# Odd attention: low keys padded with zero rows to 128, and the key latent's projection moved ahead of the compression MLP

## The chip, the cores and the metric

The kernel runs on one core of one Trainium2 chip. Its time is the device time of one execution in microseconds (us). Five engines work side by side, each through its own list of instructions in order: TensorE (PE) multiplies matrices into PSUM banks, with a second stream (PEld) that loads its weights; VectorE (DVE) and ScalarE (ACT) do the elementwise work; GpSimd (POOL) helps; SyncE (SP) issues the DMAs.

## What is computed

The program is two blocks on 256 tokens of width 1024 in fp32. Only one part of the second block is touched, the odd layer's mixer. Cut to what matters:

```python
def odd_mixer(x, w_in, w_out, cmp_pe, cmp_w1, cmp_w2, q_norm_g, kv_norm_g, w_uq, w_uk, w_uv, bias_table):
    q_c, kv_c, gate_c, cq, ckv, k_rope = split_cols(x @ w_in, ODD_SPLITS)
    q = q_c.reshape(B, S, G, Hg, C_DIM)              # G = 2 groups of Hg = 4 heads of 64
    kv = kv_c.reshape(B, S, 3, 2, G, C_DIM)
    o_cmp, slc_score = nsa_compressed(q, kv[:, :, 0, 0], kv[:, :, 0, 1], cmp_pe, cmp_w1, cmp_w2, tbl_c)
    o_slc = nsa_selected(q, kv[:, :, 1, 0], kv[:, :, 1, 1], slc_score, tbl_c)
    o_win, _ = banded_attention(q, kv[:, :, 2, 0], kv[:, :, 2, 1], WIN_SIZE - 1, tbl_c, 1)
    o_c = gates[:, :, 0] * o_cmp + gates[:, :, 1] * o_slc + gates[:, :, 2] * o_win
    qd = (rms_norm(cq, q_norm_g) @ w_uq).reshape(B, S, D_HEADS, D_NOPE + D_ROPE)
    c = rms_norm(ckv, kv_norm_g)
    k_nope, v = (c @ w_uk), (c @ w_uv)
    o_d = mla_attention(qd[..., :D_NOPE], rope(qd[..., D_NOPE:], pos), k_nope, rope(k_rope, pos), v)
    return jnp.concatenate([o_c, o_d], axis=-1) @ w_out
```

`nsa_compressed` runs a small MLP (gelu) over blocks of 32 keys, and one over blocks of 32 values, ahead of its attention.

## The kernel before

Activations lie with features on the partitions and tokens along the row. Every fp32 value that TensorE multiplies is split into a high part (rounded to the fast type) and a low part (the rest), and a product is three matmuls: high by high, low by high, high by low (L328 to L330, in `fm_mm`; L337 to L339 for the token-major form). A weight comes by DMA into a ring of raw tiles; ACT casts its high part (L320) and DVE subtracts for the low part (L321).

A scheduler places each instruction on its engine's list: of those that it reckons ready it takes the one of highest priority, and priority falls in the order in which the code makes them. The steps of the odd mixer are functions in a table, called in the order of the string `ORDER`: kv0, ks and q project keys, values and queries; c0 and c1 are the compression MLP for keys and values (`cmp_mlp`, passes L1387, its fold L1393, the last product of c0 L1408 and of c1 L1416); tm is the token-major projection of values and gates (`tmproj`); ckv projects the key latent and prepares its norm (`ckvproj`: copy L1509, then `rms_defer`, which scales on ACT, L568, squares on ACT, L491, sums the squares on PE, L454, takes the mean on ACT, L503, the power of -1/2 on POOL, L505, and spreads the result over the partitions by PE, L498); kr and cq do the same for the rotary key and the query latent (`cqproj`: copies L1522). CS0 to CS3 are the scores and softmax of pair i of heads (`c_scores`), CO0 to CO3 their outputs (`c_out`, transposes L947, products L1136 and L1138, the first of them preceded by `compressed`); uk, uv, uq are the up-projections from the latents; DS and DO the latent attention.

A score in `c_scores` is two matmuls per group g of heads and half t of the tokens. The tiles `QS[g]` hold the high part of the queries in one half of the partitions and the low part in the other; `KH[g]` holds the high keys twice, in both halves. L1468 multiplies them over 128 rows. L1469 adds high queries by low keys: the low keys KL of both groups lie in one tile, group g in its own 64 partitions, so this matmul runs over 64 rows. The columns are the keys of two branches (selected and window), 2 x 128 of them for the first half of the tokens and 2 x 256 for the second. So each pair of heads has eight matmuls, four of 256 and four of 512 columns. DVE adds the bias and takes the extreme (L1128, called from `biased`), ACT takes the exponential (L1475), DVE scales (L1484).

Tiles of the same tag share memory. The softmax of the second half (t = 1) writes tiles tagged csb1, and so do the first two weight tiles of c0 and c1: who comes later waits. The tile `te` of the query norm has the tag oks, that of KL. The query latent's tile `cq` has the tag ocq alone. PSUM has eight banks: three for projections (tag g), four for scores and transposes (tag a), one for all else (tag m).

Of the kernel before, what the change touches and what calls it, by code (L numbers as in the profile page):

```python
# [13 lines left out]
F32R = mybir.dt.float32r  # L14
# [6 lines left out]
P = 128  # L21
# [10 lines left out]
WPRI = 300  # L32
NRAW = 7
NRMS = 12
ORDER = ("kv0 ks q c0 tm ckv c1 CS0 CS1 CO0 CS2 CO1 CS3 CO2 kr CO3 cq uk uv uq DS0 DS1 DO0 DS2 DO1 DS3 "
         "DO2 DO3").split()
EORDER = ("aq av keep AS0 AS1 AO0 AO1 bq0 bq1 bq2 BS0 bv1 BS1 an bv0 bv2 BO0 BO1").split()
RA = 4
# [220 lines left out]
def _program(ctx, tc, nc, a, offs, dump):  # L259
# [17 lines left out]
    def T(pl, shape, tag, dt=F32, **k):  # L277
        cnt[0] += 1
        return pl.tile(list(shape), dt, tag=tag, name="%s_%d" % (tag, cnt[0]), **k)
# [11 lines left out]
    ident = C["ident"]  # L291
    ones = T(cp, [P, P], "ones")
    G.memset(ones, 1.0)
    mhalf = T(cp, [P, 8], "mhalf")
    G.memset(mhalf, -0.5)
    ebase = T(cp, [P, 16], "ebase")
# [2 lines left out]
    def bc(ap, shape):  # L299
        return ap.to_broadcast(list(shape))  # L300
# [1005 lines left out]
    def odd(ap_, xh, xl, W, KO, raw):  # L1306
# [1 line left out]
        X2 = T(ap_, [P, 2, 2, S], "s4")  # L1308
        X = [X2[:, j] for j in range(2)]
        KH = [T(ap_, [P, 2, S], "okh%d" % g, F32R) for g in range(2)]  # L1310
        KL = T(ap_, [P, 2, S], "oks", F32R)
        grp = (slice(0, 64), slice(64, 128))

        def evc(j, ps):
            if j == 1:
                for g in range(2):
                    for r in range(2):
                        ACT.copy(KH[g][grp[r]], ps[grp[g]])
                    tt(KL[grp[g]], ps[grp[g]], KH[g][grp[g]], op=sub)
                return  # L1320
            for u in range(2):
                V.tensor_copy(X[u][0:64, 0, :], ps[0:64, u, :])
                ACT.copy(X[u][64:128, 0, 0:S - 1], ps[0:64, u, 1:S])
                V.tensor_copy(X[u][0:64, 1, :], ps[64:128, u, :])
                ACT.copy(X[u][64:128, 1, 0:S - 1], ps[64:128, u, 1:S])
# [132 lines left out]
        def c_scores(i):  # L1458
# [4 lines left out]
            for t in range(2):  # L1463
                n = P * (t + 1)
                sps = [T(pa, [P, 2, S], "a") for g in range(2)]
                for g in range(2):
                    qt = QS[g][:, i, t * P:(t + 1) * P]
                    mm(sps[g][:, :, :n], qt, KH[g][:, :, 0:n], start=True, stop=False)  # L1468
                    mm(sps[g][:, :, :n], qt[grp[g]], KL[grp[g], :, 0:n], start=False, stop=True)  # L1469
                sb = T(ap_, [P, 2, 2, n], "csb%d" % t, bufs=2)  # L1470
                for g in range(2):
                    for b in range(2):
# [29 lines left out]
                             pT[g]) for g in range(2)], False, b == 1)  # L1502
            split(back(o), halves(yh[:, i, :]), halves(yl[:, i, :]))

        cq = T(ap_, [P, 3, S], "ocq")
        kr = T(ap_, [P, S], "okr")

        def evk(j, ps):
# [6 lines left out]
            late["k"] = rms_defer(ckv, 2, C["kv_norm"], 1e-5, ckx[:, 0], ckx[:, 1], (pg,))  # L1515

        def cqproj():
            late["cqx"] = cqx = [T(ap_, [P, 3, S], "ocx", F32R, bufs=2) for _ in range(2)]
            for n in range(3):
                ps = T(pg, [P, S], "g")  # L1520
# [279 lines left out]
```

## Time and profile before

| | us |
|---|---|
| median of 3 runs (lowest to highest) | 1218.49 (1217.42 to 1223.27) |
| the profiled execution | 1222.49 |
| its span | 1220.7 |
| PE busy in it | 1175.4 (96%) |
| DVE, ACT, POOL busy | 905.4, 681.7, 94.5 |
| the odd mixer, from the first matmul of kv0 to the final projection's last stretch | 888.28 to 999.94 |

The profile is of one execution. The span is what the profiler saw; the execution's own time has some 2 us around it. Each row of a timeline starts with its start in us from the span's begin and its length in us. A matmul's length includes the way through the array, so two matmuls that follow each other overlap: the price of one is the distance from its start to the next start. In a window's row, PEclk is the share of the full TensorE clock that was granted.

### The profile page before, as it was taken

How to read it: one execution, taken by the hardware profiler on the slowest of the kernel's cores; microseconds unless marked ns; L12 is line 12 of the kernel's file. 1: busy time of each engine (PE TensorE's matmuls, PEld its weight loads, DVE VectorE, ACT ScalarE, POOL GpSimd, SP SyncE). 2: the span in 40 equal slices, each digit the busy share in tenths (PEclk: the TensorE clock that was granted, in tenths of full speed). 3: DMA queues.
4: the chain of work that ended last, by engine and by line, in shares of the span. 5: the costliest groups of instructions: out<-in, count | busy, mean ns of one | idle time of the engine just before them, and what ended most of it. 6: DMA issues, size and time to landing. Idle time of an engine off the chain costs nothing.

```text
span 1220.7 us, 23603 instructions
## 1 busy us (share of the span) xinstructions
PE 1175.4 (96%) x9370; PEld 1111.6 (91%) x9370; DVE 905.4 (74%) x1744; ACT 681.7 (56%) x1205; POOL 94.5 (8%) x94
## 2 busy tenths in 40 slices
PE   7779999999999999999999899999999999999997
PEld 7769989999999999899998899998977789999986
DVE  8998957866689886667564886666687758976654
ACT  5345564755566765446355675554675566755541
POOL 4830000100000000000001000001000001000010
PEclk9979999999999999999999899999998999999998
DMA  7423445664356556656423556566754215666561
GB/s 262 139 87 114 147 137 179 205 202 157 100 177 196 183 177 181 196 175 215 163 79 106 170 173 187 176 181 190 261 182 139 70 54 193 208 188 188 160 201 36
DMA packets 61276, 199.41 MB, mean 163 GB/s; under 512 B 8502, under 2 KB 12398, under 8 KB 60910
## 3 DMA queue, kind: packets, MB, share of 16 engines
q1 hardware_dynamic: 54864, 191.60, 49.5%
q10 hardware_dynamic: 6302, 6.32, 1.6%
q8 instruction: 73, 1.20, 0.4%
q14 instruction: 37, 0.30, 0.1%
HBM read 196.28 MB, written 1.60 MB: 162 GB/s over the span
## 4 chain that ended last, share of the span: by engine, by line
PE 82%; DVE 11%; ACT 2%; DMA 2%; issue 2%; SPq 0%; DVEq 0%; ACTq 0%
PE g L329 10%; PE g L328 10%; PE g L330 10%; PE a L328 7%; PE a L329 7%; PE a L330 7%; PE a L393 5%; PE g L393 4%; DVE lo L321 3%; PE a L395 3%; PE g L337 2%; PE g L339 2%; PE g L338 2%; PE g L395 2%; PE a L947 1%
## 5 line engine op out<-in xcount | busy, mean ns | idle before, releaser
L321 DVE TENSOR_TENSOR lo<-raw,hi 128x1024 fp32r<-128x1024 f32 (+3 forms) x359 | 431.2, 1206 | 180.7 <-ACT hi L320 178.0
L320 ACT CAST hi<-raw 128x1024 fp32r<-128x1024 f32 (+3 forms) x359 | 363.7, 1020 | 355.4 <-PE g L329 138.8
L328 PE MATMUL g<-xh,hi 128*128 128x256 f32 (+1 forms) x616 | 176.2, 287 | 7.9 <-ACT xh L568 7.6
L329 PE MATMUL g<-xl,hi 128*128 128x256 f32 (+1 forms) x624 | 178.9, 287 | 0.3 <-DVE xl L569 0.3
L330 PE MATMUL g<-xh,lo 128*128 128x256 f32 (+1 forms) x616 | 176.3, 287 | 2.7 <-DVE lo L321 2.7
L328 PE MATMUL a<-nh,hi 128*128 128x256 f32 x560 | 159.9, 286 | 4.6 <-ACT sqa L1061 2.7
L329 PE MATMUL a<-nl,hi 128*128 128x256 f32 x560 | 159.5, 285 | 0.9 <-DVE nl L516 0.9
L330 PE MATMUL a<-nh,lo 128*128 128x256 f32 x560 | 159.3, 285 | 0.0
L328 PEld LDWEIGHTS g<-xh,hi 128*128 128x128 f32 x616 | 117.7, 191 | 9.9 <-ACT xh L568 7.9
L330 PEld LDWEIGHTS g<-xh,lo 128*128 128x128 f32 x616 | 117.4, 191 | 4.4 <-DVE lo L321 3.4
L329 PEld LDWEIGHTS g<-xl,hi 128*128 128x128 f32 x624 | 119.0, 191 | 1.4 <-DVE xl L569 0.9
L328 PEld LDWEIGHTS a<-nh,hi 128*128 128x128 f32 x560 | 108.6, 194 | 5.7 <-ACT sqa L1061 2.9
L329 PEld LDWEIGHTS a<-nl,hi 128*128 128x128 f32 x560 | 108.7, 194 | 1.1 <-DVE nl L516 1.1
L330 PEld LDWEIGHTS a<-nh,lo 128*128 128x128 f32 x560 | 108.7, 194 | 0.0
L393 PE MATMUL a<-mx,hi 128*128 128x512 f32 x264 | 91.9, 394 | 0.0
L328 PE MATMUL g<-nh,hi 128*128 128x256 f32 x288 | 81.5, 283 | 0.0
L329 PE MATMUL g<-nl,hi 128*128 128x256 f32 x288 | 81.5, 283 | 0.0
L330 PE MATMUL g<-nh,lo 128*128 128x256 f32 x288 | 81.5, 283 | 0.0
L395 PE MATMUL a<-mx,lo 128*128 128x256 f32 x264 | 73.1, 277 | 0.0
L393 PE MATMUL g<-mx,hi 128*128 128x512 f32 x198 | 69.0, 395 | 0.0
L393 PEld LDWEIGHTS a<-mx,hi 128*128 128x128 f32 x264 | 49.4, 188 | 11.5
L328 PEld LDWEIGHTS g<-nh,hi 128*128 128x128 f32 x288 | 55.3, 192 | 0.0
(619 smaller groups left out, 2905.2 us busy)
## 6 DMA issues: line engine op xcount, KB each, us to landing
raw<-g_up SPq DMA_DIRECT2D x88, 512.0 KB, 3.6
raw<-f_up SPq DMA_DIRECT2D x44, 512.0 KB, 3.5
raw<-g_dn SPq DMA_DIRECT2D x32, 512.0 KB, 3.6
raw<-w_fm SPq DMA_DIRECT2D x27, 512.0 KB, 4.1
raw<-ev_fm SPq DMA_DIRECT2D x20, 512.0 KB, 3.7
raw<-f_dn SPq DMA_DIRECT2D x16, 512.0 KB, 3.6
raw<-od_fm SPq DMA_DIRECT2D x14, 512.0 KB, 4.2
raw<-g_dn SPq DMA_DIRECT2D x16, 384.0 KB, 3.4
```

The lines of the kernel that those rows point to most:

```text
L320: ACT.copy(hi, raw)
L321: tt(lo, raw, hi, op=sub)
L328: mm(ps, hi[:, o:o + P], xh[:, k, :], start=start and k == 0, stop=False, skip_group_check=skip)
L329: mm(ps, hi[:, o:o + P], xl[:, k, :], start=False, stop=False, skip_group_check=skip)
L330: mm(ps, lo[:, o:o + P], xh[:, k, :], start=False, stop=stop and k == kt - 1, skip_group_check=skip)
L337: mm(ps, xh[:, k, t], hi[:, wsl], start=start and j == 0, stop=False, skip_group_check=skip)
L338: mm(ps, xh[:, k, t], lo[:, wsl], start=False, stop=False, skip_group_check=skip)
L339: mm(ps, xl[:, k, t], hi[:, wsl], start=False, stop=stop and j == len(ks) - 1, skip_group_check=skip)
L393: mm(f2, hi[:, o], X[:, k].rearrange("p a s -> p (a s)"), start=first and j == 0, stop=False, skip_group_check=True)
L395: mm(ps[:, 0, :], lo[:, o], X[:, k, 0, :], start=False, stop=last and j == len(ks) - 1, skip_group_check=True)
L947: PE.transpose(tr[:, k, :], b, ident)
```

## The change

Two things are changed, both in the odd mixer. First, the low keys get one tile per group (tags oks and ocq) of 128 rows, the other 64 of which ACT fills once with zeros, and L1469 multiplies the whole query tile by them, as L1468 does. Since the second of these tiles has the tag ocq, `cq` shares its memory with it, and is therefore made inside `cqproj`. Second, ckv stands ahead of c0 in `ORDER`. All lines from there on shift by two to four (L1468 is L1472 after, L498 is L500).

```diff
@@ -32,7 +32,7 @@
 WPRI = 300
 NRAW = 7
 NRMS = 12
-ORDER = ("kv0 ks q c0 tm ckv c1 CS0 CS1 CO0 CS2 CO1 CS3 CO2 kr CO3 cq uk uv uq DS0 DS1 DO0 DS2 DO1 DS3 "
+ORDER = ("kv0 ks q ckv c0 tm c1 CS0 CS1 CO0 CS2 CO1 CS3 CO2 kr CO3 cq uk uv uq DS0 DS1 DO0 DS2 DO1 DS3 "
          "DO2 DO3").split()
 EORDER = ("aq av keep AS0 AS1 AO0 AO1 bq0 bq1 bq2 BS0 bv1 BS1 an bv0 bv2 BO0 BO1").split()
 RA = 4
@@ -291,6 +291,8 @@
     ident = C["ident"]
     ones = T(cp, [P, P], "ones")
     G.memset(ones, 1.0)
+    zero = T(cp, [P, 1], "zero")
+    G.memset(zero, 0.0)
     mhalf = T(cp, [P, 8], "mhalf")
     G.memset(mhalf, -0.5)
     ebase = T(cp, [P, 16], "ebase")
@@ -1308,15 +1310,17 @@
         X2 = T(ap_, [P, 2, 2, S], "s4")
         X = [X2[:, j] for j in range(2)]
         KH = [T(ap_, [P, 2, S], "okh%d" % g, F32R) for g in range(2)]
-        KL = T(ap_, [P, 2, S], "oks", F32R)
+        KL = [T(ap_, [P, 2, S], tag, F32R) for tag in ("oks", "ocq")]
         grp = (slice(0, 64), slice(64, 128))
+        for g in range(2):
+            ACT.copy(KL[g][grp[1 - g]], bc(zero[grp[1 - g], None, :], [64, 2, S]))
 
         def evc(j, ps):
             if j == 1:
                 for g in range(2):
                     for r in range(2):
                         ACT.copy(KH[g][grp[r]], ps[grp[g]])
-                    tt(KL[grp[g]], ps[grp[g]], KH[g][grp[g]], op=sub)
+                    tt(KL[g][grp[g]], ps[grp[g]], KH[g][grp[g]], op=sub)
                 return
             for u in range(2):
                 V.tensor_copy(X[u][0:64, 0, :], ps[0:64, u, :])
@@ -1466,7 +1470,7 @@
                 for g in range(2):
                     qt = QS[g][:, i, t * P:(t + 1) * P]
                     mm(sps[g][:, :, :n], qt, KH[g][:, :, 0:n], start=True, stop=False)
-                    mm(sps[g][:, :, :n], qt[grp[g]], KL[grp[g], :, 0:n], start=False, stop=True)
+                    mm(sps[g][:, :, :n], qt, KL[g][:, :, 0:n], start=False, stop=True)
                 sb = T(ap_, [P, 2, 2, n], "csb%d" % t, bufs=2)
                 for g in range(2):
                     for b in range(2):
@@ -1502,7 +1506,6 @@
                              pT[g]) for g in range(2)], False, b == 1)
             split(back(o), halves(yh[:, i, :]), halves(yl[:, i, :]))
 
-        cq = T(ap_, [P, 3, S], "ocq")
         kr = T(ap_, [P, S], "okr")
 
         def evk(j, ps):
@@ -1515,6 +1518,7 @@
             late["k"] = rms_defer(ckv, 2, C["kv_norm"], 1e-5, ckx[:, 0], ckx[:, 1], (pg,))
 
         def cqproj():
+            cq = T(ap_, [P, 3, S], "ocq")
             late["cqx"] = cqx = [T(ap_, [P, 3, S], "ocx", F32R, bufs=2) for _ in range(2)]
             for n in range(3):
                 ps = T(pg, [P, S], "g")
```

Three places of the order of instructions. Names carry numbers that the program gives its tiles; a is a bank for scores, g one for projections, m the last one, csb softmax or MLP weights, ow the MLP's input.

TensorE, from head pair 1's last scores. Before:

```order
L1468 MATMUL a_11096<-okh_1628_10437,xh_10619 128x512
L1469 MATMUL a_11096<-oks_10438,xh_10619 128x512
L1387 MATMUL m_10988<-csb_1731_10989,ow_1650_10533 32x256 x4
L1387 MATMUL m_10988<-csb_1732_10995,ow_1650_10533 32x256 x4
L1387 MATMUL m_10988<-raw_11001,ow_1650_10533 32x256 x4
L1387 MATMUL m_10988<-raw_11007,ow_1650_10533 32x256 x3
L498 MATMUL g_10983<-consts_91,rmsr_10981 128x128 x2
L1387 MATMUL m_10988<-raw_11007,ow_1650_10533 32x256
```

After:

```order
L456 MATMUL g_10848<-ones_92,sq_1701_10849 128x1 x2
L456 MATMUL g_10848<-ones_92,sq_1702_10851 128x1 x2
L1472 MATMUL a_11099<-okh_1628_10438,xh_10623 128x512
L1473 MATMUL a_11099<-oks_10440,xh_10623 128x512
L1472 MATMUL a_11100<-okh_1629_10439,xh_10623 128x512
L1473 MATMUL a_11100<-ocq_10441,xh_10623 128x512
L500 MATMUL g_10861<-consts_91,rmsr_10859 128x128 x2
L339 MATMUL g_10914<-hi_10918,oh_10323 128x280
L340 MATMUL g_10914<-lo_10919,oh_10323 128x280
L341 MATMUL g_10914<-hi_10918,ol_10324 128x280
```

Before, c1's passes follow the scores, and the spread of the latent's rstd (L498) stands near their end; after, it follows the scores at once (L500), and the token-major projection (L339 to L341) follows it.

TensorE, around c1's last product (L1416 before, L1420 after). Before:

```order
L329 MATMUL g_11485<-ol_10322,hi_11488 128x256
L330 MATMUL g_11485<-oh_10321,lo_11489 128x256
L454 MATMUL g_11523<-ones_92,sq_1837_11524 128x1 x2
L454 MATMUL g_11523<-ones_92,sq_1838_11526 128x1 x2
L1416 MATMUL m_11031<-cod_10317,okr_11029 128x64 x2
L1453 MATMUL a_11146<-consts_91,ow_1758_11121 128x128 x2
L947 MATMUL a_11153<-consts_91,csb_1746_11043 128x128
L947 MATMUL a_11153<-consts_91,csb_1749_11058 128x128 x2
```

After:

```order
L330 MATMUL g_11458<-oh_10323,hi_11461 128x256
L331 MATMUL g_11458<-ol_10324,hi_11461 128x256
L332 MATMUL g_11458<-oh_10323,lo_11462 128x256
L1438 MATMUL a_11129<-okc_10446,s_1665_10622 128x32 x8
L1397 MATMUL m_11019<-cod_10319,okr_11017 128x32 x2
L1420 MATMUL m_11035<-cod_10319,okr_11033 128x64 x2
L1457 MATMUL a_11150<-consts_91,ow_1759_11125 128x128 x2
L949 MATMUL a_11157<-consts_91,csb_1747_11047 128x128
```

Before, 96 projection matmuls of the rotary key and query latent stand between c1's passes and this place; after, 57 of them stand ahead of c1's passes, 15 between these and this place, and 24 behind it.

ScalarE, from the latent's squares to its mean. Before (L491 squares, L503 mean):

```order
L491 ACTIVATE sq_1724_10971<-ockv_10903 128x256
L491 ACTIVATE sq_1725_10973<-ockv_10903 128x256
L1475 ACTIVATE csb_1746_11043,cden_11036<-csb_1746_11043,cnm_11035 128x128 x2
L320 CAST hi_11456<-raw_11454 128x1024
L1475 ACTIVATE csb_1746_11043,cden_11036<-csb_1746_11043,cnm_11035 128x128 x2
L1475 ACTIVATE csb_1754_11086,cden_11079<-csb_1754_11086,cnm_11078 128x128
L503 ACTIVATE rmsms_10979<-g_10970 128x2
```

After (L493 squares, L505 mean):

```order
L493 ACTIVATE sq_1702_10851<-ockv_10781 128x256
L322 CAST hi_11352<-raw_11350 128x1024
L1479 ACT_TABLE_LOAD
L1479 ACTIVATE csb_1747_11047,cden_11040<-csb_1747_11047,cnm_11039 128x128 x4
L1367 CAST xh_10623<-s_1665_10622 64x512 x2
L322 CAST hi_11429<-raw_11427 128x1024
L1479 ACTIVATE csb_1755_11090,cden_11083<-csb_1755_11090,cnm_11082 128x128
L505 ACTIVATE rmsms_10857<-g_10848 128x2
```

A cast of a weight, the load of the exponential's table, the casts of the last queries (L1367) and a second weight cast have come between the squares and the mean. Further on, the three copies of the query latent stand behind the last scores of head pair 3 on PE, because of the shared tag.

## Rows read from the trace of the kernel before

**Rows 1.** The page: the chain of work that ended last, by engine.

```profile
PE 82%; DVE 11%; ACT 2%; DMA 2%; issue 2%; SPq 0%; DVEq 0%; ACTq 0%
```

**Rows 2.** Windows: length, busy us of PE, PEld, DVE, ACT, POOL; PEclk; DMA.

```profile
888.28:905.97 17.69, 17.38 (x158) 16.13 (x157) 15.62 (x35) 12.92 (x24) 2.60 (x3) 1.00 0.67 236
909.70:923.40 13.70, 12.31 (x60) 7.24 (x60) 10.53 (x43) 9.94 (x34) 0.71 (x1) 0.50 0.57 163
938.34:962.06 23.72, 23.72 (x140) 16.40 (x140) 12.20 (x52) 15.95 (x51) 0.76 (x1) 1.00 0.20 65
962.06:978.85 16.79, 15.34 (x123) 13.62 (x122) 15.75 (x33) 7.67 (x15) 0.00 (x0) 1.00 0.39 126
978.85:999.94 21.09, 20.74 (x155) 16.54 (x155) 11.72 (x59) 13.27 (x49) 0.00 (x0) 1.00 0.08 27
692.90:701.50 8.60, 7.30 (x35) 6.95 (x36) 8.60 (x21) 4.62 (x11) 0.00 (x0) 0.61 0.35 116
```

**Rows 3.** Timeline of PE, first scores: start us, length us, line, operands.

```profile
905.97 0.28 PE L1468 MATMUL a<-okh,xh 128*128 128x256 f32 x1
906.18 0.38 PE L1469 MATMUL a<-oks,xh 64*128 64x256 f32 x1
906.50 0.39 PE L1468 MATMUL a<-okh,xh 128*128 128x256 f32 x1
...
907.12 0.49 PE L1468 MATMUL a<-okh,xh 128*128 128x512 f32 x1
907.55 0.50 PE L1469 MATMUL a<-oks,xh 64*128 64x512 f32 x1
```

**Rows 4.** Timeline of PE, 512-column matmuls; then L1468's weight loads.

```profile
951.25 0.39 PE L337 MATMUL g<-hi,xl 128*128 128x512 f32 x1
951.48 0.39 PE L338 MATMUL g<-lo,xl 128*128 128x512 f32 x1
...
L1468 PEld LDWEIGHTS a<-okh,xh x16: 186/187/333, 905.9 to 959.9; 128*128 128x128 f32 x16
```

**Rows 5.** Waits of PE, 880 to 1010: us, times, longest.

```profile
PE g L454 <- ACT sq L491: 2.2, 1, 2.2
```

**Rows 6.** Timeline of ACT and POOL, from the latent's squares to its rstd.

```profile
910.63 0.71 ACT L491 ACTIVATE sq<-ockv 128x256 f32<-128x256 f32 x2
...
914.99 0.15 ACT L503 ACTIVATE rmsms<-g 128x2 f32<-128x2 f32 x1
915.22 0.71 POOL L505 TENSOR_TENSOR rmsr<-rmsms,mhalf 128x2 f32<-128x2 f32 x1 [16.95 <-ACT rmsms L503]
```

**Rows 7.** Groups of ACT by form, 900 to 965: count, busy, mean ns.

```profile
L320 ACT CAST hi<-raw 128x1024 fp32r<-128x1024 f32 x8 | 8.4, 1044 | 7.0 <-PE g L329 4.4 <-DMA raw<-od_fm 2.5
L1475 ACT ACTIVATE csb<-csb,cnm 128x128 f32<-128x128 f32 x16 | 6.2, 392 | 0.6 <-DVE cnm L1128 0.6
L1363 ACT CAST xh<-s 64x512 fp32r<-64x512 f32 x4 | 2.5, 616 | 0.1
L1350 ACT ACT_TABLE_LOAD x1 | 1.3, 1283 | 0.0
```

**Rows 8.** Timelines of DVE, then PE: c0's input, c0's passes, c1's passes.

```profile
890.81 1.03 DVE L1339 TENSOR_TENSOR ow<-s,cod 128x240 f32<-128x240 f32 x2
893.58 1.07 PE L1387 MATMUL m<-csb,ow 128*32 128x256 f32 x16
918.71 1.93 PE L1387 MATMUL m<-csb,ow 128*32 128x256 f32 x16
```

**Rows 9.** Timeline of DVE, from the end of c1 to L1416's operand.

```profile
924.08 0.42 DVE L1390 COPY okr<-m 128x256 f32<-128x256 f32 x1 [0.25 <-PE m L1387]
...
937.17 0.29 DVE L1413 COPY okr<-ohg 128x256 f32<-128x256 f32 x1
```

**Rows 10.** Timeline of ACT, then POOL, at the query latent's norm.

```profile
938.35 0.37 ACT L1522 COPY ocq<-g 128x256 f32<-128x256 f32 x1
...
941.11 0.76 POOL L505 TENSOR_TENSOR rmsr<-rmsms,mhalf 128x2 f32<-128x2 f32 x1 [25.18 <-ACT rmsms L503]
```

## The prediction

> **What bounds the kernel now.** I read the page's chain of waits first: TensorE (PE) carries 82% of the chain that ended last [rows 1], so a change is worth what it does to PE's row of work, and the other engines count where PE stands waiting. The change touches the odd attention alone, from 888.28 us to 999.94 us, so I read that stretch by windows next [rows 2]. The reader is to see three things there. PE is busy nearly all of it: 17.38 of 17.69 us ahead of the first scores, 23.72 of 23.72 us between 938.34 and 962.06. Between 909.70 and 923.40 the granted clock is 0.50, that is 1.2 GHz instead of 2.4. And that drop has something ahead of it: the waits of PE show one wait of 2.2 us, for the squares of the key latent [rows 5], just before 911.1. A second such place lies in another stage, where from 692.90 to 701.50 the granted clock is 0.61 [rows 2]. PE being busy at 0.50 is not PE being well used: the 12.31 us of work there would be about 6.2 us at full clock.
>
> **The padding.** A score takes two matmuls into one bank, L1468 over 128 rows and L1469 over 64. From one start to the next the timeline has 0.31 us with 256 columns (906.18 to 906.50) and 0.43 us with 512 (907.12 to 907.55) [rows 3]. Two 128-row matmuls of 512 columns follow each other after 0.23 us (951.25 to 951.48) [rows 4], so half of that, 0.115 us, for 256. Each alternation between 64 and 128 rows therefore costs 0.20 us, at either size. That is as long as a weight load, 0.187 us [rows 4], which between equal shapes is hidden. With both matmuls on 128 rows I take all of it as gone: 32 matmuls by 0.20 us is 6.3 us of PE's time. The bounds are 6.3 us and nothing (the 0.20 us may belong to something else than the row count). I take the full end, since 512 and 256 columns give the same surplus and only the row count sets these pairs apart from their neighbours.
>
> The Trainium skill ("TensorE: Matmul & The Clock Gate", What overlaps and what doesn't) says the opposite of this: a weight load overlaps a running matmul only when it aims at other row groups. By that rule a padded pair, which uses all row groups, would still show its loads, and the saving would be nought; the rows speak against it, since full-row matmuls follow each other in 0.23 us with loads of 0.187 us.
>
> Its side costs: two zero fills on ACT (64 partitions by 512, which I price like the 0.62 us casts of that form [rows 7]) and one memset on POOL. ACT's order has the fills ahead of the normalisation of the odd stage, far ahead of the stretch in question, so I cost them at nothing; without that cover it is 1.2 us, once.
>
> **The key latent moved ahead of c0.** On PE's order of the changed kernel the token-major projection (48 matmuls of 280 columns, 0.128 us each by the 0.115 above, so 6.1 us) now stands behind the scores of the first two pairs of heads. So the first score comes at 905.97 - 6.1 = 899.9 us, less 0.3 us of idle that stood before the projection. Against it, c0's passes now come after 19 matmuls (890.5 us) while their input is ready at 891.84 us [rows 8]: plus 1.3 us. That gives 900.9 us. The 16 matmuls of pairs 0 and 1 take 8 x 0.115 + 8 x 0.23 = 2.8 us, and pair 1's wait for banks that VectorE empties adds up to 1.9 us (an estimate; the bound below is nothing): 905.4 us. The 2.2 us wait [rows 5] is gone, as the squares now come far earlier. On SP the two latent weights go ahead of c0's raw pieces, and the third piece of the token-major weights goes behind c1's; all these have their consumers later than before or at the same place, and I cost the reordering at nothing, with the 1.3 us above as its cover.
>
> **What is late next: the broadcast of the latent's rstd.** In the old order L498 stood behind 30 of c1's 32 passes, which began at 918.71 us [rows 8], when its operand had been ready since 915.93 us [rows 6]. In the new one it stands directly behind the scores, and the whole token-major projection waits behind it. Its operand hangs on ACT, and the squares end near 902.8 us (the projection's end at 900.3 us plus 2.5 us for one copy, two scalings, one piece of the queries and two squares). Then ACT has, ahead of the mean (L503), one 1024-wide cast 1.04, a table load 1.28, four exponentials 1.9 (0.39 each with 0.09 to read out the sum), two 0.62 casts, another 1.04 cast, one exponential 0.49 [rows 7]: 7.0 us. With 0.15 for the mean and 0.94 to the end of POOL's power [rows 6] this gives 910.9 us, against scores that end at 905.4 us: **PE idle 5.5 us**. The bound below comes from the old spacing: from the end of the squares, 911.34, to the mean, 914.99, there were 3.65 us [rows 6], which would make 907.4 us and an idle of 2.0 us.
>
> **What is late after that: c1's tail.** Behind L498 PE has 0.5 for itself and 0.5 for c0's output (estimates from two and four small matmuls), 6.1 token-major, 57 matmuls of the key rotation and query latent at 0.115 to 0.117 (6.7 us), then c1's 32 passes, 2.0 us at full clock (16 in 1.07 [rows 8]). c1 ends at 926.8 us; before it ended by 924.08, where VectorE takes its result [rows 9]. Its passes free the buffers in which the softmax of pairs 0 and 1 must write, so that softmax, c1's own tail and the compressed chain all start there. Before, 96 matmuls covered them; now 15 do. The chain from c1's end to the operand of L1416 was 13.4 us (924.08 to 937.46 [rows 9]), with three low-half subtractions in it; the new order has two fewer (2.1 us, priced like the 1.04 us casts of the same halves [rows 7]), and L1393 comes some five matmuls of 0.115 us sooner. I take 10.7 us: L1416 at 937.5 us, against 938.34. PE idles some 7 us in it; the bounds are 13.4 us of chain (940.2) and 9 us (935.8, without one pair's four exponentials of 0.39 us).
>
> **And third: the query latent's norm.** Its tile now shares a slot with the second padded key tile, so its three copies (L1522) wait for the last score of pair 3. Before, the last copy was at 938.35 and the rstd ready at 941.87 [rows 10], long before it was wanted. Now copies, squares and norm lie between the last score and the up-projections uk, uv, uq. From L1416, pairs 2 and 3 cost some 15 us: the old stretch to 960.8 us was 22.4, less 5.6 for uk and uv that no longer interleave (24 matmuls of 256 columns, 12 of 512), less 3.1 for 16 alternations, plus 2.8 for 24 matmuls of the query latent, less what scores waited for. That is 952.5 us. The norm then takes up to 9.6 us (on ACT three copies, three scalings, three squares, and exponentials and copies of the outputs between them, some 19 instructions at 0.37 to 0.49 us [rows 7, 10], 8.4 us; the mean and POOL's power 1.2), with 4.5 us of the transposes and outputs of pairs 2 and 3 beside it: uk starts at 962 us, at best at 957. Then uk, uv 5.6 and uq 8.4 us and about 2 for what stands between: D's scores at 978.1 us against 978.85 [rows 2]. In the old D stretch of 21.09 us [rows 2] PE also had the remnants of pair 3's output and more of the final projection, which the new order puts earlier; I take 3.8 us off. **Sum without the clock: 0.7 + 3.8 = 4.5 us less than before.**
>
> **The clock.** The old order's 2.2 us wait was followed by 1.2 GHz [rows 2, 5]. Three idles of 5.5, about 7 and about 5 us now stand at its place, so I expect the same behind each. What it costs: the shorter example lost half of 7.30 us of PE's work, 3.65 us, the longer one half of 12.31, 6.15 us [rows 2]. The second idle is followed by a stretch that the softmax chain paces, where a slow PE costs little. I count two losses of 3.65 us: -4.5 + 7.3 = +2.8 us. The profiled execution took 1222.49 us with a span of 1220.7; the median of the runs is 1218.49, and I lay the difference on that: **1221 us**.
>
> **Rivals.** *The refund stays* (faster): the idles come out at their lower bounds (2.0 instead of 5.5, nothing of the third) and the clock does not fall after them. Then -4.5 - 3.5 less what one idle hides of the next, about -8.5 us: 1210 us. For it: PE's old wait was the only one in the stage [rows 5]. Against it: even that one of 2.2 us was followed by half the clock.
> *The clock falls long* (slower): each of the first and third idles is followed by a stretch like 909.70 to 923.40, at 6.15 us: -4.5 + 12.3 = +7.8, 1226 us. It decides from two such stretches on; three make 1232 us. For it: there PE was busy and stayed at 0.50 for 13.7 us.
> *The padding saves nothing* (the change doesn't do what it says): the pair's 0.20 us is not due to the rows. The stretches in which PE waits hide half of the 6.3 us, so +2.8 + 3.1: 1224 us. For it: a weight load as long as the surplus can be exposed between equal shapes too, when the tiles differ. Against it: the 0.23 us of full-row neighbours, whose weights differ as well [rows 4]. The Trainium skill's rule on weight loads, told above, would end here.
>
> **How the numbers follow.** Forecast 0.45; the refund stays 0.25; the clock falls long 0.20; padding saves nothing 0.10. What a measurement can tell from no change is 0.5%, 6.1 us: under 1212.4 is faster, over 1224.6 slower. The first rival is faster (0.25), the clock rival slower (0.20), the last one half each way (0.05), and of the forecast's share 0.03 reaches over the line: slower 0.28, same 0.47. The range goes from the refund rival's 1209 to 1230 us, between one and two more long stretches of half clock.
>
> **What would show it.** Right: score pairs at 0.115 and 0.23 us; a wait of PE at the rstd's broadcast of 2 to 6 us that ends with ACT's mean or POOL's power; L1416's operand ended last by VectorE with PE idle ahead of it; the copies of the query latent behind pair 3's last score; a PEclk under 1 behind these. Wrong: pairs still at 0.31 and 0.43; a PE without waits between 900 and 965 us; the odd stage ending more than 6 us from 999.94 in either direction.

## The result, and the profile after

| | before | after |
|---|---|---|
| median of 5 runs, us | 1218.49 | 1230.6 |
| lowest to highest | 1216.95 to 1223.27 | 1229.41 to 1233.03 |
| ratio of the runs, with its 95% interval | | 1.0101 (1.008 to 1.0122) |
| span of the profiled execution | 1220.7 | 1228.8 |
| odd stage in it, from the first matmul on the normalised input to the final projection's last stretch | 888.28 to 999.78: 111.5 | 885.37 to 1007.90: 122.5 |

The change makes the kernel 1.0% slower, 12.1 us. The odd stage alone is 11.0 us longer. It starts 2.9 us sooner in the profiled execution, which is no work of the change: the same instructions ahead of it met another clock, here in one window of the kernel before and then of the kernel after (columns as in [rows 2]):

```profile
623.00:627.00 4.00, 4.00 (x23) 4.00 (x23) 2.43 (x9) 2.23 (x5) 0.43 (x1) 0.57 0.16 60
```

```profile
623.00:627.00 4.00, 4.00 (x37) 4.00 (x36) 2.58 (x10) 2.96 (x6) 1.64 (x1) 1.00 0.17 66
```

A place of this kind near 700 us makes up the rest. So below I count from the start of the stage in each kernel (888.28, 885.37); "+13.0" means 13.0 us after it.

The chain of waits of the kernel after has the same shape as [rows 1], with more of PE:

```profile
PE 87%; DVE 8%; ACT 3%; issue 2%; DMA 1%; POOL 0%; SPq 0%; DVEq 0%; ACTq 0%
```

What differs is the list of PE's waits in the stage (line, releaser, us in total, times, longest). Before, the longest was the 2.2 us of [rows 5]. After:

```profile
PE m L1420 <- DVE okr L1417: 7.3, 1, 7.3
PE g L500 <- POOL rmsr L507: 6.0, 1, 6.0
PE m L1138 <- ACT epT L1504: 1.5, 1, 1.5
...
PE g L456 <- ACT sq L493: 0.5, 1, 0.5
```

The windows of the stage (length, then busy us of PE, PEld, DVE, ACT and POOL, PEclk, DMA share, GB/s) put each wait beside what the clock did, as [rows 2] did for the kernel before:

```profile
903.40:909.35 5.95, 0.01 (x1) 0.01 (x1) 3.41 (x6) 5.75 (x22) 1.30 (x1) 0.67 0.29 88
909.35:912.26 2.91, 2.91 (x13) 2.91 (x14) 0.29 (x2) 0.37 (x1) 0.00 (x0) 0.50 0.57 180
931.00:938.34 7.34, 0.01 (x2) 0.03 (x1) 7.31 (x33) 1.75 (x5) 0.00 (x0) 0.62 0.38 121
938.34:942.98 4.64, 4.64 (x21) 4.35 (x21) 2.57 (x7) 1.81 (x4) 0.00 (x0) 0.50 0.00 0
955.80:963.46 7.66, 5.62 (x40) 3.86 (x40) 5.34 (x20) 7.44 (x26) 0.00 (x0) 1.00 0.00 0
963.46:970.29 6.83, 6.83 (x32) 5.79 (x33) 1.80 (x6) 2.44 (x7) 0.70 (x1) 0.50 0.01 2
986.65:1007.90 21.25, 21.03 (x154) 17.50 (x153) 12.61 (x61) 13.43 (x47) 0.00 (x0) 1.00 0.24 72
```

The reader is to see two stretches in which PE does nothing (0.01 us busy of 5.95, 0.01 of 7.34), a third in which it is busy 5.62 of 7.66, and behind each of the three a stretch at 0.50. Together those stretches hold 2.91 + 4.64 + 6.83 = 14.4 us of PE at 1.2 GHz. I estimate that the clock took half of that, 7.2 us. The kernel before had 12.31 us of PE at 0.50 in the stage [rows 2], by the same estimate 6.2 us.

The padding itself does on PE what was forecast. The timeline of the scores (start, length, line, operands), where [rows 3] had distances of 0.31 and 0.43 us:

```profile
946.32 0.28 PE L1472 MATMUL a<-okh,xh 128*128 128x256 f32 x1
946.44 0.28 PE L1473 MATMUL a<-ocq,xh 128*128 128x256 f32 x1
946.56 0.40 PE L1472 MATMUL a<-okh,xh 128*128 128x512 f32 x1
946.80 0.39 PE L1473 MATMUL a<-oks,xh 128*128 128x512 f32 x1
```

From 946.32 to 946.44 is 0.12 us, from 946.56 to 946.80 0.24 us. Not every score comes to that: behind an output product of 64 columns (L1138 and L1140, 128*64 in the view) the first distance is still 0.23 us with 256 columns (953.66 to 953.89) and 0.34 with 512 (955.13 to 955.47).

### The profile page after: what moved, and what is told of

Same layout as the page of the kernel before. It is cut to its first block, busy times and chain, and to the rows that moved or that the text cites. A ratio compares the mean times of both kernels' runs of the same rounds, so it can differ in the third digit from the quotient of the medians.

```text
span 1228.8 us, 23607 instructions
## 1 busy us (share of the span) xinstructions
PE 1168.0 (95%) x9370; PEld 1109.3 (90%) x9370; DVE 904.6 (74%) x1744; ACT 683.4 (56%) x1207; POOL 91.7 (7%) x95
## 4 chain that ended last, share of the span: by engine, by line
PE 87%; DVE 8%; ACT 3%; issue 2%; DMA 1%; POOL 0%; SPq 0%; DVEq 0%; ACTq 0%
PE g L331 12%; PE g L332 12%; PE g L330 12%; PE a L330 7%; PE a L331 7%; PE a L332 7%; PE a L395 5%; PE g L395 4%; PE a L397 2%; PE g L341 2%; PE g L340 2%; PE g L339 2%; DVE lo L323 2%; PE g L397 2%; PE a L949 1%
## 5 line engine op out<-in xcount | busy, mean ns | idle before, releaser
L323 DVE TENSOR_TENSOR lo<-raw,hi 128x1024 fp32r<-128x1024 f32 (+3 forms) x359 | 429.0, 1200 | 182.4 <-ACT hi L322 178.5
```

The source lines that it names most:

```text
L323: tt(lo, raw, hi, op=sub)
```

## The experiments

Ten kernels were run, each timed in rounds beside the kernel before on the same chip; its median there was 1217.4 to 1220.1 us, so the ratios are what is to be compared.

| kernel | ckv ahead of c0 | low keys | ratio to before (95%) | c1 ends at | stage ends at | PE at 0.50, us |
|---|---|---|---|---|---|---|
| before | no | 64 rows | 1 | +35.4 | +111.5 | 12.3 |
| after | yes | 128, shared with cq | 1.0101 (1.008 to 1.0122) | +41.1 | +122.5 | 14.4 |
| e1 | no | 128, shared with cq | 1.0054 (1.003 to 1.0078) | +30.1 | +113.8 | 17.0 |
| e2 | no | 128, free rows | 0.9963 (0.9948 to 0.9979) | +28.9 | +104.9 | 6.8 |
| e3 | yes | 64 rows | 1.0093 (1.0072 to 1.0115) | +42.5 | +120.6 | 18.4 |
| e4 | yes | 128, free rows | 1.0044 (1.0021 to 1.0067) | +41.9 | +115.0 | 9.1 |
| e5 | yes, norm behind c1 | 128, free rows | 1.001 (0.9994 to 1.0026) | +33.8 | +107.3 | 3.0 |
| e6 | yes, c1 ahead of tm | 128, free rows | 1.011 (1.0071 to 1.0149) | +33.5 | +119.3 | 17.1 |
| e9 | no, norm late | 128, free rows | 0.9999 (0.9987 to 1.0012) | +35.4 | +110.6 | 15.5 |
| e10 | yes, c1's weights in the ring | 128, free rows | 1.0047 (1.0024 to 1.007) | +36.3 | +113.6 | 10.8 |
| e11 | no, norm late, ring | 128, free rows | 0.9985 (0.9964 to 1.0005) | +27.8 | +105.6 | 8.3 |
| e12 | no | 64 rows, low products side by side | 0.9995 (0.9975 to 1.0014) | +31.4 | +109.1 | 13.7 |

"c1 ends" is the start of its last pass on PE; the last column is PE's busy time in the stage while the granted clock was 0.50. The last three columns are of one profiled execution each, whose time differs from the median by up to 5 us.

**The two parts and the shared memory apart: e1 to e4.** The theory: the padding gains, and what the move and the shared memory add are waits. e1 is the change with the old order of steps:

```diff
-ORDER = ("kv0 ks q ckv c0 tm c1 CS0 ...
+ORDER = ("kv0 ks q c0 tm ckv c1 CS0 ...
```

> The padding as in the change, with the second low-key tile sharing the memory of the query latent, but the order of the steps as before (ckv behind tm). Theory (the time went to waits that the move and the shared memory made, the padding itself gains): score pairs at 0.115 and 0.23 us, about 3 us gained in the pairs 0 and 1 and no wait for the rstd's broadcast behind them; but the query latent's copies still stand behind pair 3's last score, so 6 to 9 us are lost there: 1218.5 - 3 + 7, about 1222 us (1219 to 1226). Rival (the move alone costs, the shared memory is harmless): 1213 us. Rival (the padding gains nothing anywhere): 1225 us or more.

e2 keeps the old order and lays both low-key tiles into the half of the key latent's tile (tag xl) that nobody uses; `cq` and `te` have their memory as before:

```diff
-        KL = [T(ap_, [P, 2, S], tag, F32R) for tag in ("oks", "ocq")]
+        KL = []
...
             if j == 1:
+                late["big"] = T(hp, [P, 8, S], "xl", F32R)
                 for g in range(2):
+                    KL.append(late["big"][:, 4 + 2 * g:6 + 2 * g, :])
...
-            ckx = late["ckx"] = T(hp, [P, 2, 2, S], "xl", F32R)
+            ckx = late["ckx"] = late["big"][:, 0:4, :].rearrange("p (a k) s -> p a k s", a=2)
```

> The padding alone, with both low-key tiles in rows that the key latent's tile leaves free, so that neither the query latent nor the query norm's product waits for them; the order of the steps as before. The zero fills stand inside the odd stage, on ACT. Theory: the whole gain of the padding without its cost, 32 x 0.2 = 6.3 us less what DVE and ACT set in the pairs: 1212 to 1215 us, no wait of PE for the query latent's norm. Rival (the padding saves nothing on the path, since the softmax chain paces the pairs): 1217 to 1220 us.

e3 is the kernel before with the new `ORDER` and nothing else:

```diff
-ORDER = ("kv0 ks q c0 tm ckv c1 CS0 ...
+ORDER = ("kv0 ks q ckv c0 tm c1 CS0 ...
```

> The move of ckv ahead of c0 alone, the low keys on 64 rows in one tile as before. Theory: the waits of PE for the rstd's broadcast (6 us) and for c1's tail (7 us less three score pairs' time) are there, the one for the query latent's norm is not: +3 to +7 us, 1222 to 1226 us. Rival (all of the loss comes from the move): 1230 us. Rival (all comes from the shared memory): 1216 to 1219 us.

e4 is e2 with the new order of steps, that is the change with the low keys laid elsewhere:

```diff
-ORDER = ("kv0 ks q c0 tm ckv c1 CS0 ...
+ORDER = ("kv0 ks q ckv c0 tm c1 CS0 ...
```

> The change with the move, and the low-key tiles in rows of the key latent's tile, so that only the shared memory is taken away. Theory: the first two waits stay (6 and 7 us), the third goes with its late up-projections, 8 to 10 us: 1220 to 1223 us. Rival (the norm is late anyway, the shared memory costs nothing): 1229 to 1232 us.

In us of the 1217.5 that the kernel before took beside them (each within some 3 us by its interval): e2 -4.5, e1 +6.6, e3 +11.3, e4 +5.4; the kernel after, by its ratio, +12.3. So the padding in free rows is worth 4.5 us in the old order and 5.9 (e3 to e4) in the new one; the move costs 11.3 without the padding and 9.9 with it; the shared memory costs 11.1 in the old order and 6.9 in the new one. 11.3 for the move, less 5.9 for the padding, plus 6.9 for the shared memory is 12.3 again, since the steps lead from the one kernel to the other. e1's 1223.7 lies near the 1222 expected, e2's 1212.4 in its range of 1212 to 1215, e4's 1223.2 at the end of its range. e3's 1228.6 is above its 1222 to 1226 and nearer to its rival's 1230: the move alone was dearer than its waits.

The waits were not all as expected either. PE's long wait for c1's tail, 7.3 us in the kernel after and 3.5 in e1, is in neither e3 nor e4, where some 7 us of it were expected. The longest waits of e4 are:

```profile
PE g L500 <- POOL rmsr L507: 8.4, 2, 6.0
PE m L1499 <- DVE oyl L518: 2.3, 1, 2.3
```

So the move alone does not make that wait; it stands where the low keys share memory with the query latent.

These prices have the clock in them, and its part is large. In the windows of the half clock, e1 (the first three rows below) had 17.0 us of PE there and e2 (the last two) 6.8:

```profile
908.67:915.50 6.83, 6.81 (x43) 4.73 (x46) 4.35 (x22) 5.17 (x20) 1.69 (x1) 0.50 0.44 138
932.57:935.98 3.41, 3.41 (x17) 3.12 (x17) 1.95 (x4) 1.81 (x4) 0.00 (x0) 0.50 0.28 109
956.46:963.29 6.83, 6.83 (x32) 5.73 (x32) 1.75 (x7) 2.59 (x7) 0.70 (x1) 0.50 0.01 2
```

```profile
906.17:909.58 3.41, 3.41 (x18) 2.11 (x22) 1.86 (x7) 3.41 (x14) 0.72 (x1) 0.50 0.41 143
930.06:933.47 3.41, 3.41 (x19) 3.41 (x18) 1.77 (x4) 1.28 (x4) 0.00 (x0) 0.50 0.14 53
```

Half the difference of that column is an estimate of the clock's part: 5.1 us of the 8.9 by which e1's stage is longer than e2's, 4.7 of the 5.6 between e3 and e4, 2.7 of the 7.5 between e4 and the kernel after, 2.7 of the 6.6 that e2's stage gains on the kernel before. All timed executions together point the same way: one less the granted clock, times the span, is on average 18.2 us in e2, 23.5 in e1, 20.8 in e4, 24.6 in the kernel after and 26.1 in e3 (idle time counted too). So each part's effect on the whole time is shown, and how it divides between waits, work and clock is an estimate from one profile each.

The shared memory shows in e1 as it was forecast: the timeline of ACT has the three copies of the query latent waiting for the last low product, and the mean follows 8.6 us later.

```profile
949.05 0.92 ACT L1526 COPY ocq<-g 128x256 f32<-128x256 f32 x3 [1.61 <-PE a L1473]
...
957.67 0.17 ACT L505 ACTIVATE rmsms<-g 128x2 f32<-128x2 f32 x1 [0.88 <-PE g L456]
```

Its waits have one more: c1 ends sooner here, and PE waits for c1's tail, since 24 matmuls of the query latent, whose banks wait for those copies, stand behind it now.

```profile
PE m L1420 <- DVE okr L1417: 3.5, 1, 3.5
```

In e4 the wait for the rstd's broadcast is there to the tenth of a microsecond, 5.96 us. In e3, with dearer scores, it is 1.4 us, and the broadcast starts at the same place as in e4 and in the kernel after, +24.0 to +24.1 us. Timelines of PE, of e3 and then of e4:

```profile
909.67 1.22 PE L498 MATMUL g<-consts,rmsr 128*128 128x128 f32 x4 [1.41 <-POOL rmsr L505]
```

```profile
904.10 0.40 PE L1475 MATMUL a<-xl,xh 128*128 128x512 f32 x1
910.47 1.22 PE L500 MATMUL g<-consts,rmsr 128*128 128x128 f32 x4 [5.96 <-POOL rmsr L507]
```

So up to that broadcast the padding buys nothing in the new order: what it takes from the scores goes into the wait, and the chain over ACT and POOL sets the time. What e4 gains on e3 comes behind it, from the shorter half clock and from pairs 2 and 3.

**Where the move's price sits: e5, e6, e10.** e5 makes the key latent's norm a step of its own, called behind c1:

```diff
-            late["k"] = rms_defer(ckv, 2, C["kv_norm"], 1e-5, ckx[:, 0], ckx[:, 1], (pg,))
+        def ckvnorm():
+            late["k"] = rms_defer(late["ckv"], 2, C["kv_norm"], 1e-5, late["ckx"][:, 0], late["ckx"][:, 1], (pg,))
...
-ORDER = ("kv0 ks q ckv c0 tm c1 CS0 ...
+ORDER = ("kv0 ks q ckv c0 tm c1 kn CS0 ...
```

> As e4 (move, padded keys in free rows), but the key latent's norm is a step of its own behind c1, so that the scheduler no longer puts the rstd's broadcast straight behind the scores: the token-major projection stands ahead of them. Theory (the 6 us wait for the broadcast sits on the path): that wait goes with its 1.2 us of half clock, 1215 to 1219 us. Rival (c1's late tail sets the stretch, PE only waits elsewhere): within 2 us of e4's 1223.

1.0010 against e4's 1.0044: 4.1 us less, and the stage 7.7 us shorter in the profiles. The token-major projection now stands ahead of the scores, and the longest wait for a broadcast is 1.6 us.

The theory holds in its direction and in the range (1218.8 of 1215 to 1219). But the edit also brought c1 forward, from +41.9 to +33.8 us, and PE's time at 0.50 fell from 9.1 to 3.0 us, so it does not say whether the idle, its clock or the late c1 is what costs. e6 was to tell this, with c1 ahead of tm in `ORDER` and the wait left in:

```diff
-ORDER = ("kv0 ks q ckv c0 tm c1 CS0 ...
+ORDER = ("kv0 ks q ckv c0 c1 tm CS0 ...
```

> As e4, but c1 ahead of the token-major projection in the order of steps, so that c1's passes come some 8 us sooner with more projection matmuls behind them. The 6 us wait for the broadcast stays. Theory (c1's tail, which frees the softmax of the second halves, is the second part of the move's price): 1214 to 1219 us. Rival (the broadcast's wait is the whole price of the move): 1221 to 1224 us.

It was slower, 1.0110; neither theory had that. c1 did come forward to +33.5 us; but the gates come out of the token-major projection, their tile was copied only at 937.26 us (+50.9; in e4 at +37.7, in e2 at 907.87, +25.0), and the softmax's last step needs them. Pair 2's scores started at +68.0 instead of e4's +61.6 us. Rows of DVE, of e6 and of e2, at the copy of the gates:

```profile
937.26 0.19 DVE L1361 COPY ogt<-m 128x48 f32<-128x48 f32 x1
```

```profile
907.87 0.20 DVE L1361 COPY ogt<-m 128x48 f32<-128x48 f32 x1
```

The late gates are not the whole of it. DVE then made 16 softmax scalings in a row, and in the same microseconds POOL's power for the query latent lasted 4.47 us, against 0.70 to 2.09 for every other power in the stage of these kernels; PE waited 4.8 us for it. Rows of DVE and POOL in e6:

```profile
938.16 3.75 DVE L1490 TENSOR_SCALAR csb<-csb,cden 128x128 f32<-128x128 f32 x16
```

```profile
938.33 4.47 POOL L507 TENSOR_TENSOR rmsr<-rmsms,mhalf 128x2 f32<-128x2 f32 x1 [28.32 <-ACT rmsms L505]
```

And PE had 17.1 us at 0.50 against e4's 9.1, by the estimate above 4.0 us of the 4.3 by which e6's stage is longer. So e6 does not decide between the two theories.

e10 takes c1's weights out of the memory that the softmax of the second halves uses:

```diff
-                    w1 = T(ap_, [P, 4 * 256], "csb1", bufs=2) if qr < 2 else T(wr, [P, 4 * 256], "raw")
+                    w1 = T(ap_, [P, 4 * 256], "csb1", bufs=2) if qr < 2 and u == 0 else T(wr, [P, 4 * 256], "raw")
```

> As e4, but c1's first two weight tiles lie in the ring of raw weights instead of in the memory of the softmax of the second halves, so this softmax no longer waits for c1's passes; the scheduler then also puts c1 ahead of the rotary key and query latent. The 6 us wait for the broadcast stays. Theory (the shared memory of c1's weights and the softmax makes the late tail dear): 1212 to 1218 us. Rival (only the order of c1 and the projections counts): same as e6.

No gain (1.0047 against 1.0044), which neither expectation had: c1 ended 5.6 us sooner than in e4 and PE did not wait for its tail, but the ring of raw weights was now two tiles shorter for what follows, and PE waited for cast weights instead:

```profile
PE g L330 <- ACT hi L322: 5.7, 2, 3.5
PE g L500 <- POOL rmsr L507: 4.0, 1, 4.0
```

So this run shows a new wait beside the one for the broadcast, not that the shared memory was harmless.

**A version that beats both, and its bounds: e9, e11, e12.** e2 is faster than the kernel before, by 0.4%. It still waits 1.4 us for the squares of the key latent. e9 is e2 with the norm as a step of its own, as in e5, called late; e11 is e9 with c1's weights in the ring, by e10's edit:

```diff
-ORDER = ("kv0 ks q c0 tm ckv c1 CS0 CS1 CO0 CS2 CO1 CS3 CO2 kr CO3 cq ...
+ORDER = ("kv0 ks q c0 tm ckv c1 CS0 CS1 CO0 CS2 CO1 CS3 CO2 kr CO3 kn cq ...
```

> As e2 (padding without the move, low keys in free rows), and the key latent's norm as a step of its own ahead of the query latent's, so that matmuls of the rotary key stand ahead of its sums on PE. Theory (e2's wait of 1.4 us for the squares and the fall of the clock behind it are on the path): 1209 to 1211 us. Rival (the softmax behind c1 sets the end of that stretch): 1212 to 1214 us, as e2.

> The padding without the move (as e2), with c1's weights in the raw ring and the key latent's norm as a late step of its own. Theory: e2's wait for the latent's squares (1.4 us) goes and with it the fall of the clock behind it (about 1.8 us), so 1212.4 - 3 = 1209 us (1206 to 1211). Rival (the ring of raw weights, two tiles shorter for c1, makes later weights late): 1213 us or more.

Both theories missed: 0.9999 and 0.9985. e9 lies above its rival's range too; e11's 1215.1 is what its rival had. In e9 the scheduler filled the place of the sums with 24 projection matmuls, and c1's last pass went from +28.9 to +35.4 us; the stage ended 5.7 us later. Of these, some 4.3 us are the clock's by the estimate above (15.5 us of PE at 0.50 against 6.8), so that the late c1 is what cost is not shown. In e11 c1 came early (+27.8), and PE waited 1.9 us for cast weights and 1.7 us for the broadcast instead.

e12 asks what the 0.20 us per product belongs to. It is the kernel before with the loops of a score split:

```diff
                     mm(sps[g][:, :, :n], qt, KH[g][:, :, 0:n], start=True, stop=False)
+                for g in range(2):
+                    qt = QS[g][:, i, t * P:(t + 1) * P]
                     mm(sps[g][:, :, :n], qt[grp[g]], KL[grp[g], :, 0:n], start=False, stop=True)
```

> The kernel before, without padding and without the move; only the loops of a score are written so that both groups' high products come first and both low products after them, and in pair 0 the two 64-row products then stand side by side, group 0 in the lower and group 1 in the upper 64 rows. Theory (the 0.20 us belongs to each change between 64 and 128 rows): in pair 0 high to high 0.115 us (0.23 at 512 columns), low to low 0.115 us or less, and the surplus of 0.20 us only where high turns to low or back; by the Trainium skill (TensorEngine Tiling (Array Packing), Key Properties: tiles operate independently) the two low products would even run at the same time. Total 1215 to 1218 us. Rival (a 64-row product is dear by itself): low to low 0.31 us as before, 1217 to 1219 us.

In pair 0 the low products of the two groups do stand side by side there. The timeline of PE (x2: two instructions in the row):

```profile
901.92 0.40 PE L1468 MATMUL a<-okh,xh 128*128 128x256 f32 x2
902.25 0.39 PE L1471 MATMUL a<-oks,xh 64*128 64x256 f32 x2
902.57 0.73 PE L1468 MATMUL a<-okh,xh 128*128 128x512 f32 x2
903.23 0.51 PE L1471 MATMUL a<-oks,xh 64*128 64x512 f32 x2
```

From the first of the two high products to the two low ones 0.33 us, from the two low ones to the next high one 0.32 us. A single low product between high ones took 0.31 us [rows 3]; two side by side take the same 0.32 together, and the row of the two is 0.39 us long against 0.38 for one [rows 3], so they start 0.01 us apart or less. So a 64-row product is not dear by itself: it is the turn from 128 to 64 rows and back that costs, and two low products in different halves of the rows run at the same time, as the Trainium skill has it (TensorEngine Tiling (Array Packing), Key Properties). The total did not move, 0.9995: only in pair 0 did the scheduler leave the low ones side by side.

## Why the prediction was wrong, point by point

It forecast 1221 us, no measurable change, with a range up to 1230; the kernel takes 1230.6. The mechanisms were those of its sum, but for the D stretch and for what makes PE wait for c1's tail; the sizes of several later terms were off. By its steps, in us from the start of the stage; the forecast is the sum without the clock's losses (it added 7.3 us for these at the end), the measured times have them in (by the estimate 1.5 us by 912.26, 3.8 by 942.98, 7.2 by 970.29, from the windows above):

| place | forecast | measured |
|---|---|---|
| first score | +12.6 | +13.0 |
| broadcast of the key latent's rstd (idle ahead of it) | +22.6 (5.5) | +24.0 (5.97) |
| L1416, now L1420 (idle ahead of it) | +49.2 (7) | +53.0 (7.33) |
| last score of pair 3 | +64.2 | +70.1 |
| up-projection starts | +73.7 | +83.7 |
| first score of D | +89.8 | +101.3 |
| end of the stage | +107.0 | +122.5 |

**The padding's price on PE**: right, as the timelines show. Of the 6.3 us that it was to take off the time, 4.5 came off in the old order (e2) and 5.9 in the new one (e3 to e4), in both with a part that is the clock's; up to the broadcast nothing came off in the new one. The Trainium skill's rule weighed against it ("TensorE: Matmul & The Clock Gate", What overlaps and what doesn't, by which a full-row weight load could not hide) falls for this kernel: full-row scores with loads of 0.187 us [rows 4] follow each other after 0.12 us.

**The move, the broadcast, c1's tail**: both waits are there, each with its releaser and nearly its size, 5.97 and 7.33 us of idle against 5.5 and about 7. The second was put down to the move's order alone; e3 and e4 have that order and no such wait, so it needs the shared memory as well, by which 24 matmuls of the query latent stand behind it. Of the chain over ACT the timeline shows all that was summed, the squares' end at 901.35, the table load, and the mean 6.4 us later:

```profile
900.94 0.41 ACT L493 ACTIVATE sq<-ockv 128x256 f32<-128x256 f32 x1
...
902.30 1.28 ACT L1479 ACT_TABLE_LOAD   x1
...
907.76 0.15 ACT L505 ACTIVATE rmsms<-g 128x2 f32<-128x2 f32 x1
```

The power on POOL then took 1.30 us instead of the 0.71 of [rows 6]. Rows of POOL and DVE:

```profile
907.99 1.30 POOL L507 TENSOR_TENSOR rmsr<-rmsms,mhalf 128x2 f32<-128x2 f32 x1 [16.00 <-ACT rmsms L505]
```

```profile
907.50 1.22 DVE L323 TENSOR_TENSOR lo<-raw,hi 128x1024 fp32r<-128x1024 f32 x1 [0.30 <-ACT hi L322]
```

It ends 0.57 us after DVE's low-half subtraction does (909.29 against 908.72). So it does in e1, where the power took 1.69 us, and in e9, where it took 1.68; the query latent's power in the kernel after, with DVE idle, took 0.70. The broadcast was 1.4 us later than forecast because the squares ended 1.5 us later (+16.0 instead of +14.5), ACT came from there to the mean 0.6 us faster (6.4 instead of 7.0), and POOL was 0.6 us slower. (The forecast also had the mean's 0.15 us twice: the 0.94 us of [rows 6] counts from the mean's start.)

**The query latent's norm**: the mechanism is right, the wait behind the last low product is there, and e1 against e2 and the kernel after against e4 show what it costs: 11.1 and 6.9 us. The forecast had 9.5 us from the last score to the up-projection; it took 13.6, of which the clock took some 2.8. The norm itself had the forecast's length: 9.5 us from the first copy to the end of POOL's power at 965.43, against 9.6. But PE, which stood idle for 2.0 us and not for about 5, was then at half clock with transposes and outputs of pair 3 until 968.35, where the broadcast began: these did not all fit beside the norm.

```profile
955.90 0.92 ACT L1526 COPY ocq<-g 128x256 f32<-128x256 f32 x3 [1.60 <-PE a L1473]
...
964.48 0.17 ACT L505 ACTIVATE rmsms<-g 128x2 f32<-128x2 f32 x1 [0.83 <-PE g L456]
```

```profile
964.73 0.70 POOL L507 TENSOR_TENSOR rmsr<-rmsms,mhalf 128x2 f32<-128x2 f32 x1 [55.44 <-ACT rmsms L505]
```

**The D stretch, the 3.8 us taken off, is the step that failed outright.** I reckoned that the new order had put more of the final projection ahead of it. It is the other way round. The groups of PE in that stretch, of the kernel before (978.68, its first score, to 999.78) and of the kernel after (986.65 to 1007.90):

```profile
L329 PE MATMUL g<-oyl,hi 128*128 128x256 f32 x17 | 4.9, 311 | 0.0
L330 PE MATMUL g<-oyh,lo 128*128 128x256 f32 x17 | 4.7, 302 | 0.0
L328 PE MATMUL g<-oyh,hi 128*128 128x256 f32 x16 | 3.6, 303 | 0.0
L1136 PE MATMUL m<-epT,ovs 128*64 128x256 f32 x8 | 1.9, 398 | 0.0
```

```profile
L331 PE MATMUL g<-oyl,hi 128*128 128x256 f32 x21 | 5.9, 294 | 0.0
L330 PE MATMUL g<-oyh,hi 128*128 128x256 f32 x22 | 5.7, 305 | 0.0
L332 PE MATMUL g<-oyh,lo 128*128 128x256 f32 x21 | 5.6, 280 | 0.0
```

Before, 50 matmuls of the final projection and pair 3's outputs stood there; after, 64 and none of pair 3's. The stretch is 21.25 us long; before it was 21.10. The old order had slipped 16 projection matmuls between the up-projections, where pair 3's outputs stood in the new one.

**The clock** came out at the right size, 7.2 us against 7.3, in part by luck: the forecast was two losses of 3.65 us, the profile has three, of 1.5, 2.3 and 3.4 by estimate, and the largest lay behind the shortest idle. The 3.65 were half of all 7.30 us of PE's work in a window at 0.61, of which only a part stood at 0.50. The rival that would have been nearest in time, the clock falling for long, has the wrong reason: the half-clock stretches of PE were short, 2.9 to 6.8 us against 12.3. The rival that the change gains fell with the idles; the rival that the padding saves nothing is refuted by the distances of 0.12 and 0.24 us and by e2.

So of the 15.5 us between the forecast's +107.0 and the measured +122.5, the clock is 7.2, the D stretch 4.0, and the rest, some 4.3, is spread: with the clock taken out, the broadcast was 1.4 us late, L1420 another 0.9, the way from the last score to the up-projection was 1.3 us longer and that from there to D's first score 0.9, while pairs 2 and 3 came to their sum. The forecast counted 7.3 for the clock, so the stage was some 8 us short. The total was 9.6 us short, since the medians lie 12.1 us apart and the profiled stages 11.0.

**What stays open.** How the move's 9.9 us divide between PE's idle ahead of the broadcast, the late c1 and the clock. In the kernels whose low keys share no memory and whose gates come early (e2, e4, e5, e9, e10, e11) the end of the stage goes with c1's end: +27.8 and +28.9 give +105.6 and +104.9, +33.8 gives +107.3, +35.4 and +36.3 give +110.6 and +113.6, +41.9 gives +115.0. That is an order, not a proof, since each edit moved other things too; the one meant to move c1 alone (e6) held the gates back. The clock makes a good part of it: less half of PE's time at 0.50, the three kernels without the move (e2, e9, e11) end at +101.4 to +102.9, wherever c1 ends, and the three with it at +105.8 to +110.5.

## What to carry to other kernels

A tile that borrows memory brings its last reader with it: ask who waits for that reader, and what of the next step hangs behind. With the shared memory the padding made the kernel 6.6 us slower in the old order, in rows that were free 4.5 us faster. A step moved forward brings its slowest small chain with it (here squares, mean, power, broadcast over four engines); if its result is needed late, call the chain as a late step, and ask first what stood in line behind the old place. And before a difference between two kernels is put down to their waits, compare what each had of the half clock.

## What the runs showed of the hardware

The turn between 64-row and 128-row products costs PE 0.20 us each way (0.31 and 0.43 us from start to start where scores alternate [rows 3], 0.12 and 0.24 where all have 128 rows), and two 64-row products in different halves of the rows, side by side, start 0.01 us or less apart and take the time of one (e12). And the clock can fall without a long wait ahead of it. In e3, PE had waited 0.76 us at most in the stage and was busy by the profile, with nine scores in 3.3 us that alternate between 64 and 128 rows, when the clock went to half; in e4, with full-row scores, it was at full clock through the same place and fell only within the 6 us wait. Windows of e3, then of e4:

```profile
898.70:902.00 3.30, 3.28 (x9) 1.66 (x9) 3.09 (x15) 3.24 (x8) 0.00 (x0) 1.00 0.54 165
902.00:907.90 5.90, 5.90 (x16) 3.71 (x15) 3.75 (x13) 5.82 (x14) 0.00 (x0) 0.51 0.23 74
```

```profile
898.00:904.50 6.50, 5.21 (x31) 3.92 (x29) 6.22 (x27) 6.33 (x12) 0.00 (x0) 1.00 0.42 156
904.50:910.47 5.97, 0.01 (x2) 0.01 (x1) 3.43 (x6) 5.77 (x22) 1.30 (x1) 0.78 0.25 88
```

So the prediction's reading that the 2.2 us wait of [rows 5] brought the clock down in the kernel before is not shown: there too alternating scores stood just ahead of it. Nor did each idle cost alike: behind 5.95 us of idle PE had 2.91 us at half clock, behind 7.34 us 4.64, and in the third place, with PE busy 5.62 of 7.66 us, 6.83 us. POOL's power on one 128x2 tile took 0.70 us with DVE idle. Where a low-half subtraction of DVE (L323) lay over its start, it ended 0.57 us after that, in the kernel after, e1 and e9 alike. The 4.47 us beside e6's 16 scalings fit this, but no run shows that DVE is the cause there.
